# A hybrid streaming encoder step on one core: other assumed times in the scheduler that orders its instructions

## The chip, the core and the metric

The kernel runs on one core of a Trainium2 chip. The metric is the device time of one execution in microseconds (us), the median of several runs. A core has five engines that run beside each other, each through its own instructions in a fixed order: PE (TensorE, the matmuls; PEld is its loading of weights), DVE (VectorE), ACT (ScalarE), POOL (GpSimd) and SP (SyncE, which here issues nearly all DMAs). An instruction that needs another engine's result waits on a semaphore, and what stands behind it on its own engine waits with it.

## The reference, cut to what matters

One layer (DEPTH is 1) over 64 new frames of a running stream and over 16 meta tokens and 2048 prompt frames of a new one, 1024 features wide:

```python
hn = rms_norm(x, prm['norm_mix_g'][l])
proj = hn @ prm['w_in'][l]
aq, ak, av, lx, lg, gq, gk, gv, glr, gog = jnp.split(proj, split_points, axis=-1)
...
o_att = diff_attention_prompt(q, k.reshape(b, L, ATT_HEADS, 2, ATT_DH), v, lam)
...
hseq, lru_h1 = rg_lru(xc, lru_h0, ...)
o_lru = hseq * jax.nn.gelu(lg)
...
o_gla, S1 = gla_blocked(...)
o_gla = rms_norm(o_gla.astype(dt), prm['gla_norm_g'][l]).reshape(b, L, GLA_VW) * jax.nn.silu(gog)
x = x + jnp.concatenate([o_att, o_lru, o_gla], axis=-1) @ prm['w_out'][l]
hn = rms_norm(x, prm['norm_ffn_g'][l])
u = hn @ prm['ffn_w_up'][l]
uc, ffn_c1 = causal_dwconv(u, ffn_c0, prm['ffn_conv_w'][l], prm['ffn_conv_b'][l])
x = x + (jax.nn.gelu(uc) * (hn @ prm['ffn_w_gate'][l])) @ prm['ffn_w_down'][l]
```

A final norm follows. Differential attention has 4 heads with two score maps each (exponentials, normalised, one subtracted from the other), and its keys reach back over all chunks. The LRU and the gated linear attention (GLA) are recurrences along the frames. The feed-forward part (FFN) is 2816 wide.

## The kernel before

**Layout.** Features lie on the partitions and the 2128 frames in the columns. Each large matmul is done as three products in a rounded 32-bit type: high part by high part, high by low, low by high (names end in h and l, or hi and lo). So each weight tile `raw` must first be split: ACT rounds it to `whi` (L154), and POOL (L261) or DVE (L160) takes the difference `wlo`. That happens on first use; both parts are then stored in DRAM (`WS`) and read back for later groups of columns.

**Three streams** are written by generators that take turns in `Flow.run` in fixed shares (1680, 564 and 640), which makes the order of the program's text:

- dense: the input projection in six blocks of columns (`ps_w`, L645 and L647), each with a norm ahead of it; then the FFN in four groups of columns, 512, 512, 512 and 336+256. A group is the output projection (`pd`, L1435), the residual add with a sum of squares, a norm, then per FFN tile the products up and gate (`pu`, `pg`, L1302), the convolution and GELU on DVE, ACT and POOL (L1314 to L1339), the rounding to `gh` (L157), and the product down (`pd`, L1369) with the add to x on DVE (L1375).
- attention: the scores of a unit (`ps_sc`, L1056 to L1063), their minimum on DVE (L1065) and the exponential on ACT (L1066), in two PSUM buffers; a mixing of the two maps (`pc`: a multiply on POOL, L157, then one on DVE, L1104, that also adds); and PV: transposes (`ps_pt`, L1155), a split into `ph` (ACT, L154) and `pl` (DVE, L160), the products with V (`ps_o`, L1170), and a norm over each head (`osq`, `ps_on`, `dgt`, L1185 to L1196). Its instructions have a priority 500 ahead of dense.
- recurrent: LRU (L712 to L767) and GLA (L789 to L960), also 500 ahead.

A group of the FFN may begin only when the attention and recurrent chunks that it needs are done. Between the last product down of one group and the output projection of the next, TensorE also runs the final norm of the first of them. The last group (336+256) runs when both mixers are through.

**A norm** is the same chain everywhere: squares summed by a matmul (`ps_sq`, L397), a multiply-add on DVE (L420), a power on POOL (L421), a diagonal matrix `dg` on DVE (L426), and a matmul that spreads it over the partitions (`ps_nb`, L432). Then come y (DVE, L439), its rounding to `h2h` (ACT, L154) and the difference `h2l` (DVE L160 or POOL L444), on which the next matmuls of dense wait. What keeps TensorE busy meanwhile is work of the two mixers that stands between L397 and the next dense matmul:

```python
for w, a, b in runs(cuts):
    nc.vector.tensor_scalar(r[:w, a:b], ps[:w, a:b], 1.0 / D, EPS, ALU.mult, ALU.add)
nc.gpsimd.tensor_tensor(out=r[:, :len(cuts)], in0=r[:, :len(cuts)], in1=mhalf[:, :len(cuts)], op=ALU.pow)
```

**What sets the order on the engines** is not the text alone. The program is built under `tile.TileContext(nc, schedule_with_timeline_sim=True)`. That scheduler runs through the program on assumed times: on each engine, of the instructions whose inputs are there by its assumed clock, it places the one with the best priority (the place in the text, less 500 for the mixers, 50000 for a norm of the FFN, 100000 for the setup). The result is one fixed list of instructions for each engine with its waits. At run time nothing is reordered. The assumed times come from a table of constants, `TRN2Spec`: `CYCLE_T` holds the nanoseconds of one cycle of DVE, ACT and POOL, and `PE_FULL_CLOCK_PASS_GAP_NS` (2.5 before) is what a matmul takes beyond one column for each cycle at the full clock.

## Time and profile before

| | |
|---|---|
| median of 3 runs | 2969.09 us (2964.97 to 2972.47) |
| profiled execution, its own time | 2967.71 us |
| its span in the trace | 2965.9 us |
| mean granted TensorE clock | 0.98 |
| busy: PE, DVE, ACT, POOL | 2840.8, 1892.6, 1097.0, 759.3 us |
| DMA | 669.92 MB, mean 226 GB/s |

The span runs from the first to the last instruction on the slowest core (here the only one); the time of the execution holds 1.8 us more. Busy time of PE counts its pipelined matmuls with modelled ends, so that it also holds time in which TensorE ran at half clock or drained between dependent steps.

### The profile page before, as it was taken

To read this page: it belongs to the slowest core of one execution; us is meant where nothing else is said; L and a number is where in the kernel's file an instruction comes from. 1 tells how busy PE (TensorE), PEld (TensorE's weight loads), DVE (VectorE), ACT (ScalarE), POOL (GpSimd) and SP (SyncE) were. 2 spreads that over 40 slices of the span, in tenths; PEclk is the share of its full clock that TensorE was granted. 3 is DMA by queue.
4 is the path that set the end of the run, shared out by engine and by line. 5 is a ranking of instruction groups with operands and counts; after the bars stand their busy time and mean duration, and the time that the engine had idled before them with its cause. 6 is when DMAs were issued, how large, how long until landed. Compare 5 with 4: busy or idle time off the path is not lost.

```text
span 2965.9 us, 44899 instructions
## 1 busy us (share of the span) xinstructions
PE 2840.8 (96%) x16031; PEld 2501.3 (84%) x16031; DVE 1892.6 (64%) x3798; ACT 1097.0 (37%) x2525; POOL 759.3 (26%) x1162
## 2 busy tenths in 40 slices
PE   6998999999899999998999999999999999999998
PEld 6988999999777877877787888877888889999998
DVE  6467656564578898899687687766565445433334
ACT  5344443442444454554343343334332112211112
POOL 4224312221245445444222212223021101100001
PEclk9998999999899999999999999999999999999999
DMA  9997677787967787887575665685555764434443
GB/s 327 324 272 215 228 259 218 234 272 229 337 234 252 262 277 255 263 263 246 196 236 187 202 210 194 217 288 192 195 193 191 259 219 156 171 142 171 146 167 134
DMA packets 314942, 669.92 MB, mean 226 GB/s; under 512 B 35127, under 2 KB 174143, under 8 KB 314719
## 3 DMA queue, kind: packets, MB, share of 16 engines
q1 hardware_dynamic: 314574, 667.05, 67.1%
q8 instruction: 127, 2.08, 0.3%
q14 instruction: 97, 0.79, 0.1%
q10 hardware_dynamic: 144, 0.01, 0.0%
HBM read 491.99 MB, written 174.96 MB: 225 GB/s over the span
## 4 chain that ended last, share of the span: by engine, by line
PE 48%; DVE 5%; DMA 2%; POOL 1%; issue 1%; ACT 1%; SPq 0%; POOLq 0%; ACTq 0%; DVEq 0%
PE pd L1369 13%; PE pg L1302 12%; PE pu L1302 12%; PE pd L1435 4%; PE ps_o L1170 2%; DMA whi<-WS 2%; PE ps_pt L1155 1%; PE ps_sc L1063 1%; PE ps_sc L1056 1%; DVE pc L1104 1%; POOL pc L157 1%; DVE y L439 0%; PE ps_r L895 0%; DVE cc L1326 0%; DVE x L1375 0%
## 5 line engine op out<-in xcount | busy, mean ns | idle before, releaser
L1066 ACT ACTIVATE pc<-ps_sc,NB 128x512 f32<-128x512 f32 (+6 forms) x400 | 224.1, 562 | 298.2 <-DVE NB L1065 284.4
L1369 PE MATMUL pd<-gh,whi 128*128 128x512 f32 (+2 forms) x880 | 319.0, 366 | 11.0 <-DVE x L1375 5.0
L1302 PE MATMUL pu<-h2h,whi 128*128 128x512 f32 (+2 forms) x880 | 318.9, 362 | 6.9 <-DVE cc L1337 4.5
L1302 PE MATMUL pg<-h2h,whi 128*128 128x512 f32 (+2 forms) x880 | 317.3, 361 | 4.7 <-DMA whi<-WS 3.6
L1302 PE MATMUL pu<-h2l,whi 128*128 128x512 f32 (+2 forms) x880 | 317.0, 360 | 0.5 <-DVE h2l L160 0.4
L1302 PE MATMUL pg<-h2l,whi 128*128 128x512 f32 (+2 forms) x880 | 316.3, 359 | 0.0
L1302 PE MATMUL pu<-h2h,wlo 128*128 128x512 f32 (+2 forms) x880 | 316.2, 359 | 0.0
L1302 PE MATMUL pg<-h2h,wlo 128*128 128x512 f32 (+2 forms) x880 | 315.2, 358 | 0.0
L1369 PE MATMUL pd<-gh,wlo 128*128 128x512 f32 (+2 forms) x880 | 313.0, 357 | 0.0
L1369 PE MATMUL pd<-gl,whi 128*128 128x512 f32 (+2 forms) x880 | 312.9, 358 | 0.0
L1375 DVE TENSOR_TENSOR x<-x,pd 128x512 f32<-128x512 f32 (+2 forms) x360 | 222.4, 623 | 139.1 <-PE pd L1369 136.6
L1326 DVE SCALAR_TENSOR_TENSOR cc<-uh,prm,cc 128x512 f32<-128x512 f32 (+4 forms) x264 | 174.7, 667 | 180.2 <-ACT cc L1324 176.8
L1065 DVE TENSOR_REDUCE NB<-ps_sc 128x1 f32<-128x512 f32 (+6 forms) x400 | 208.2, 530 | 102.3 <-PE ps_sc L1063 101.0
L645 PE MATMUL ps_w<-hh,whi 128*128 128x384 f32 (+2 forms) x768 | 260.7, 341 | 12.6 <-ACT whi L154 9.7
L645 PE MATMUL ps_w<-hh,wlo 128*128 128x384 f32 (+2 forms) x768 | 261.2, 341 | 8.7 <-DVE wlo L160 5.3
L645 PE MATMUL ps_w<-hl,whi 128*128 128x384 f32 (+2 forms) x768 | 258.0, 337 | 0.0
L1319 ACT ACTIVATE uh<-pu 128x512 f32<-128x512 f32 (+4 forms) x132 | 59.2, 463 | 382.5 <-PE pu L1302 381.0
L261 POOL TENSOR_TENSOR wlo<-raw,whi 128x1024 fp32r<-128x1024 f32 (+2 forms) x63 | 151.6, 2407 | 169.8 <-ACT whi L154 152.0
L1369 PEld LDWEIGHTS pd<-gh,whi 128*128 128x128 f32 x880 | 165.5, 189 | 34.8 <-DVE x L1375 7.5
L1302 PEld LDWEIGHTS pu<-h2h,whi 128*128 128x128 f32 x880 | 167.7, 191 | 29.5 <-DVE cc L1337 5.3
L157 POOL TENSOR_SCALAR gh<-cc 128x512 fp32r<-128x512 f32 (+4 forms) x132 | 68.7, 523 | 483.5 <-DVE cc L1339 299.5
L157 POOL TENSOR_SCALAR pc<-pc,fr 128x512 f32<-128x512 f32 (+4 forms) x200 | 159.1, 813 | 123.7 <-DVE fr L1086 106.2
(330 smaller groups left out, 6975.6 us busy)
## 6 DMA issues: line engine op xcount, KB each, us to landing
whi<-WS SPq DMA_DIRECT2D x276, 512.0 KB
wlo<-WS SPq DMA_DIRECT2D x276, 512.0 KB
WS<-whi SPq DMA_DIRECT2D x94, 512.0 KB
WS<-wlo SPq DMA_DIRECT2D x94, 512.0 KB
Kc<-KHL SPq DMA_DIRECT2D x48, 512.0 KB
V<-VHL SPq DMA_DIRECT2D x48, 512.0 KB
Q<-QHL SPq DMA_DIRECT2D x64, 256.0 KB
raw<-in_wu SPq DMA_DIRECT2D x22, 512.0 KB
```

The costliest lines, as they stand in the source:

```text
L157: nc.gpsimd.tensor_scalar(out, in_, s, 1.0, ALU.mult, ALU.mult)
L261: nc.gpsimd.tensor_tensor(out=lo[:, :n], in0=t[:, :n], in1=f(hi[:, :n]), op=ALU.subtract)
L645: nc.tensor.matmul(ps[:, :n], lhsT=wx, rhs=hx, start=st_, stop=sp_)
L1065: nc.vector.tensor_reduce(NB[:qw, ti, m, ci:ci + 1], ps[:qw, :kt_], AX.X, ALU.min)
L1066: nc.scalar.activation(out=pv_[m][:qw, :kt_], in_=ps[:qw, :kt_], func=AF.Exp, scale=-1.0, bias=NB[:qw, ti, m, ci:ci + 1], accum_out=SS[:qw ...
L1170: nc.tensor.matmul(oT, lhsT=V[:kw, b0 // P, a, :], rhs=r[:kw, i, :], start=(first and i3 == 0), stop=(fin and i3 == 2))
L1302: nc.tensor.matmul(ps[:, :n], lhsT=w_[wi_][:, k * P:(k + 1) * P], rhs=hx, start=(k == 0 and i3 == 0), stop=(k == KT - 1 and i3 == 2))
L1319: nc.scalar.activation(out=uh[:, 2:2 + m], in_=pu[:, a:b], func=AF.Copy)
L1326: nc.vector.scalar_tensor_tensor(out=cc[:, :m], in0=uh[:, w:w + m], scalar=cw[w], in1=cc[:, :m], op0=ALU.mult, op1=ALU.add)
L1369: nc.tensor.matmul(ps[:, :n], lhsT=w_, rhs=g_[:, o:o + n], start=(j == 0 and i3 == 0), stop=(j == len(gts) - 1 and i3 == 2))
L1375: nc.vector.tensor_tensor(x2[b, ct], x2[b, ct], ps[:, :n], ALU.add)
L1435: nc.tensor.matmul(ps[:, :n], lhsT=w_, rhs=g_, start=(k == 0 and i3 == 0), stop=(k == KT - 1 and i3 == 2))
```

## The change

Ahead of everything else, the module now writes four numbers of the scheduler's table: the cycle of DVE 1.4 times as long as it was, that of ACT 1.15 times, that of POOL 1.2 times, and 13 ns in place of 2.5 beyond the columns of a matmul. Nothing else differs, and every later line has a number 9 higher.

```diff
+from concourse.hw_specs import TRN2Spec
 from concourse.masks import make_identity
+
+
+TRN2Spec.CYCLE_T = {
+    mybir.EngineType.DVE: 1.4 * TRN2Spec.CYCLE_T[mybir.EngineType.DVE],
+    mybir.EngineType.Activation: 1.15 * TRN2Spec.CYCLE_T[mybir.EngineType.Activation],
+    mybir.EngineType.Pool: 1.2 * TRN2Spec.CYCLE_T[mybir.EngineType.Pool],
+}
+TRN2Spec.PE_FULL_CLOCK_PASS_GAP_NS = 13.0
```

Both programs hold the same instructions (15731 rows of PE in either). What differs is the order on each engine. Written as a difference of the two lists, 4787 rows of PE, 2957 of DVE, 1638 of ACT, 560 of POOL and 779 of SP stand elsewhere, most of them by a few places. Three places follow, of the kernel before and then of the changed one.

**ScalarE at the start.** The input projection's first column blocks run here: `whi` is the rounding of a weight tile that TensorE waits for, `sp_b` and `l1p` belong to the setup of the LRU, `sq` to the squares of the next block's norm, `acc` (L407, L416) to its end, `ckr` to the cached keys. Before:

```order
L349 ACTIVATE l1p<-sp_b 128x2
L154 ACTIVATE whi<-raw 128x1024
L154 ACTIVATE ckr<-ck 128x512
L154 ACTIVATE whi<-raw 128x1024
L407 ACTIVATE acc<-ps_nb 128x384
L712 ACTIVATE xc<-lx,prm 128x83
L154 ACTIVATE hh_0_346<-y 128x384 x3
L154 ACTIVATE whi<-raw 128x1024
```

And changed:

```order
L347 ACTIVATE sp_b<-sp_b 128x2
L391 ACTIVATE sq<-xt 128x384
L163 ACTIVATE whi<-raw 128x1024
L358 ACTIVATE l1p<-sp_b 128x2
L163 ACTIVATE ckr<-ck 128x512
L163 ACTIVATE whi<-raw 128x1024
L721 ACTIVATE xc<-lx,prm 128x83
L163 ACTIVATE whi<-raw 128x1024
L736 ACTIVATE tt<-ps_r,hb 128x83
L743 ACTIVATE tt<-tt,nsp_192 128x83
L416 ACTIVATE acc<-ps_nb 128x384
```

The last `whi` shown stands ahead of `acc` and of four steps on `hh` where it stood behind them, and the first one stands ahead of `l1p`.

**GpSimd at the final norm of the second FFN group,** ahead of the output projection of the third (about 1955 us in the trace before). `r_20961` and `dgt` belong to the norm of an attention head, `r` with L421 (L430) is the dense stream's norm, `pc` the mixing of the attention's two maps. Before:

```order
L214 TENSOR_SCALAR r_20961<-r_20961 128x2
L215 TENSOR_TENSOR r_20961<-r_20961,mhalf 128x2
L157 TENSOR_SCALAR dgt<-ident,r_20961 128x128 x2
L421 TENSOR_TENSOR r<-r,mhalf 128x4
L157 TENSOR_SCALAR pc<-pc,fr 128x512 x6
L157 TENSOR_SCALAR pc<-pc,fr 128x384 x2
L157 TENSOR_SCALAR pc<-pc,fr 128x16
L157 TENSOR_SCALAR pc<-pc,fr 128x144
```

And changed:

```order
L223 TENSOR_SCALAR r_20961<-r_20961 128x2
L224 TENSOR_TENSOR r_20961<-r_20961,mhalf 128x2
L166 TENSOR_SCALAR dgt<-ident,r_20961 128x128 x2
L166 TENSOR_SCALAR pc<-pc,fr 128x512 x6
L166 TENSOR_SCALAR pc<-pc,fr 128x384 x2
L166 TENSOR_SCALAR pc<-pc,fr 128x16
L166 TENSOR_SCALAR pc<-pc,fr 128x144
L430 TENSOR_TENSOR r<-r,mhalf 128x4
```

Ten mixings that stood behind the dense norm's power now stand ahead of it.

**TensorE at the same norm.** `ps_sq` (L397, L406) sums the squares, `ps_nb` (L432, L441) spreads the result, `pd` (L1435, L1444) is the next dense step; the rest is attention and GLA. Before:

```order
L1063 MATMUL ps_sc<-Kc,Q 128x144
L1056 MATMUL ps_sc<-Kc,Q 128x144
L1061 LDWEIGHTS mq
L1061 MATMUL ps_sc<-mk,mq 128x64
L1063 MATMUL ps_sc<-Kc,Q 128x144
L1185 MATMUL ps_on<-ones,osq 128x1 x2
L397 MATMUL ps_sq<-ones,acc 128x1 x4
L1194 MATMUL ps_on<-dgt,ones 128x256
L432 MATMUL ps_nb<-dg,ones 128x512
L1435 MATMUL pd<-h2h_20338,whi 128x512
```

And changed (`ps_sq` stands eleven rows above the first row shown):

```order
L923 MATMUL ps_r<-S_p,qkd 128x256
L925 MATMUL ps_r<-gvr,att 128x64 x4
L1179 MATMUL ps_o<-pl,V 128x256
L1179 MATMUL ps_o<-ph,V 128x256 x2
L1179 MATMUL ps_o<-pl,V 128x256
L1164 MATMUL ps_pt<-ident,pc 128x128 x4
L1065 MATMUL ps_sc<-Kc,Q 128x512
L1072 MATMUL ps_sc<-Kc,Q 128x512
L930 MATMUL ps_r<-gvr,qkd 128x256
L441 MATMUL ps_nb<-dg,ones 128x512
L1444 MATMUL pd<-h2h_20338,whi 128x512
```

Nineteen rows of attention and GLA stand between `ps_sq` and `ps_nb`, where before one stood there.

**TensorE at the second norm of the last group** (about 2507 us), where no mixer is left. `pu` and `pg` are the group's first up and gate products over its block of 336 columns; the norm is that of its block of 256. Before:

```order
L432 MATMUL ps_nb<-dg,ones 128x256
L432 MATMUL ps_nb<-dg,ones 128x80
L397 MATMUL ps_sq<-ones,acc 128x1 x2
L1302 MATMUL pu<-h2h_24682,whi 128x336
L1302 MATMUL pg<-h2h_24682,whi 128x336
L1302 MATMUL pu<-h2l_24683,whi 128x336
L1302 MATMUL pu<-h2h_24682,wlo 128x336
L1302 MATMUL pu<-h2h_24682,whi 128x336
```

And changed:

```order
L441 MATMUL ps_nb<-dg,ones 128x256
L441 MATMUL ps_nb<-dg,ones 128x80
L406 MATMUL ps_sq<-ones,acc 128x1 x2
L1311 MATMUL pu<-h2h_24682,whi 128x336
L1311 MATMUL pg<-h2h_24682,whi 128x336
L441 MATMUL ps_nb<-dg,ones 128x256
L1311 MATMUL pu<-h2l_24683,whi 128x336
L1311 MATMUL pu<-h2h_24682,wlo 128x336
```

The `ps_nb` of the block of 256 columns stands two matmuls behind its `ps_sq`; before, 26 matmuls stand between them.

## Rows read from the trace of the kernel before

**Rows 1.** The page: busy time of each engine, two of its lines of 40 slices (tenths; 9 is 90% or more), and the shares of the chain of waits by engine.

```profile
PE 2840.8 (96%) x16031; PEld 2501.3 (84%) x16031; DVE 1892.6 (64%) x3798; ACT 1097.0 (37%) x2525; POOL 759.3 (26%) x1162
...
PEclk9998999999899999999999999999999999999999
DMA  9997677787967787887575665685555764434443
...
PE 48%; DVE 5%; DMA 2%; POOL 1%; issue 1%; ACT 1%; SPq 0%; POOLq 0%; ACTq 0%; DVEq 0%
```

**Rows 2.** The chain of waits in order of time, in the last quarter: start, duration, work: 24 matmuls of 512 columns.

```profile
2338.63 5.44 PE pu L1302 x24
```

**Rows 3.** Windows of the core: stretch in us, its length, then busy us and instructions of PE, PEld, DVE, ACT and POOL, the granted clock, the DMA share, GB/s. The first goes from the end of the input projection to the first output projection; the others hold the norm ahead of the FFN in group 0, the final norm of group 0, the norm ahead of the FFN in group 1, the final norm of group 1, and the norm ahead of the FFN in group 2.

```profile
768.00:804.00 36.00, 27.76 (x121) 21.10 (x121) 23.34 (x48) 16.24 (x41) 8.95 (x14) 0.72 1.01 365
846.00:864.00 18.00, 12.51 (x48) 8.26 (x47) 16.19 (x41) 8.06 (x20) 9.95 (x13) 0.77 0.86 277
1381.00:1395.00 14.00, 12.07 (x81) 10.34 (x79) 13.86 (x42) 7.29 (x22) 2.58 (x3) 1.00 0.63 200
1448.00:1462.00 14.00, 13.74 (x88) 11.79 (x87) 12.05 (x26) 10.39 (x25) 5.42 (x8) 1.00 0.56 179
1951.00:1963.00 12.00, 7.43 (x32) 5.11 (x30) 9.83 (x24) 3.38 (x12) 7.81 (x12) 0.67 0.76 221
2018.00:2029.00 11.00, 10.12 (x66) 7.96 (x65) 7.71 (x18) 6.38 (x18) 1.22 (x2) 1.00 0.51 157
```

**Rows 4.** The same view of the start, and of the rest of the input projection.

```profile
27.00:75.00 48.00, 33.38 (x166) 30.58 (x167) 38.07 (x76) 22.98 (x44) 28.71 (x29) 0.85 0.92 311
75.00:110.00 35.00, 31.97 (x180) 31.01 (x179) 10.73 (x23) 11.36 (x20) 8.49 (x4) 0.86 0.99 342
110.00:760.00 650.00, 630.34 (x4201) 599.28 (x4200) 391.14 (x933) 273.45 (x746) 169.96 (x264) 0.99 0.78 249
```

**Rows 5.** The timeline of PE: the last matmul of the projection and the first of the output projection of group 0.

```profile
768.65 0.28 PE L645 MATMUL ps_w<-hh,wlo 128*128 128x256 f32 x1
...
797.77 0.63 PE L1435 MATMUL pd<-h2h,whi 128*128 128x512 f32 x1
```

**Rows 6.** What scores (L1056) and PV (L1170) waited for on TensorE over the whole span: us in total, times, the longest.

```profile
PE ps_o L1170 <- DVE pl L160: 8.1, 8, 2.9
PE ps_sc L1056 <- ACT pc L1066: 7.9, 11, 2.7
PE ps_o L1170 <- ACT ph L154: 6.6, 6, 2.5
```

**Rows 7.** The timeline of ACT at the start (start, duration, line, work, and in brackets the idle time ahead of it and what ended it), then a row of PE there.

```profile
32.21 0.20 ACT L349 ACTIVATE l1p<-sp_b 128x2 f32<-128x2 f32 x1 [4.20 <-DVE sp_b L346]
...
73.17 0.34 ACT L753 ACTIVATE lgt<-lgt 128x160 f32<-128x160 f32 x1 [1.58 <-DVE lgt L752]
73.42 0.87 ACT L154 ACTIVATE whi<-raw 128x816 fp32r<-128x816 f32 x1
...
74.34 0.51 PE L647 MATMUL ps_w<-whi,hh 128*80 128x272 f32 x1 [5.16 <-ACT whi L154]
```

**Rows 8.** The timeline at the final norm of the second group: POOL, then PE.

```profile
1955.01 0.19 POOL L214 TENSOR_SCALAR r<-r 128x2 f32<-128x2 f32 x1 [7.03 <-DVE fr L1080]
...
1956.79 1.02 POOL L421 TENSOR_TENSOR r<-r,mhalf 128x4 f32<-128x4 f32 x1
1957.80 7.73 POOL L157 TENSOR_SCALAR pc<-pc,fr 128x512 f32<-128x512 f32 x10
...
1952.04 0.23 PE L1056 MATMUL ps_sc<-Kc,Q 128*128 128x144 f32 x1
...
1954.62 1.58 PE L397 MATMUL ps_sq<-ones,acc 128*128 128x1 f32 x8
...
1961.29 2.07 PE L432 MATMUL ps_nb<-dg,ones 128*128 128x512 f32 x2 [3.19 <-DVE dg L426]
1962.37 1.41 PE L1435 MATMUL pd<-h2h,whi 128*128 128x512 f32 x1
```

**Rows 9.** The timeline at the second norm of the last group: PE, DVE, POOL.

```profile
2506.65 0.61 PE L397 MATMUL ps_sq<-ones,acc 128*128 128x1 f32 x4 [0.58 <-DVE acc L384]
...
2513.65 0.59 PE L432 MATMUL ps_nb<-dg,ones 128*128 128x256 f32 x2
...
2511.69 0.47 DVE L426 TENSOR_SCALAR dg<-ident,r 128x128 f32<-128x128 f32 x2
...
2509.32 0.98 POOL L421 TENSOR_TENSOR r<-r,mhalf 128x2 f32<-128x2 f32 x1
```

**Rows 10.** Groups by line and shape: names, shapes, count, busy us, mean ns of one, idle us before them. First DVE: the minimum of a score step, the mixing, and a step of the FFN's convolution that multiplies and adds on the same shape. Then ACT: the exponential of a score step.

```profile
L1065 DVE TENSOR_REDUCE NB<-ps_sc 128x1 f32<-128x512 f32 x192 | 129.5, 683 | 45.2 <-PE ps_sc L1063 44.8
...
L1104 DVE SCALAR_TENSOR_TENSOR pc<-pc,fr 128x512 f32<-128x512 f32 x96 | 95.2, 1022 | 8.4 <-POOL pc L157 8.2
...
L1339 DVE SCALAR_TENSOR_TENSOR cc<-uh,cc 128x512 f32<-128x512 f32 x44 | 30.2, 687 | 2.2
...
L1066 ACT ACTIVATE pc<-ps_sc,NB 128x512 f32<-128x512 f32 x192 | 131.3, 685 | 160.3 <-DVE NB L1065 157.0 <-DVE dg L862 2.8
```

## The prediction

> **What bounds the kernel now.** I read the page first. [rows 1] PE is busy 96% of the span and leads the chain of waits; no other engine passes 64%, and DMA is full only in the first quarter. So the time is TensorE's: its streaming, plus what it loses in waits and at half clock. The chain in order of time shows the streaming undisturbed [rows 2]: 24 matmuls of 512 columns in 5.44 us, 226.7 ns each. At the upper clock of 2.4 GHz 512 columns are 213.3 ns, so 13.3 ns stand beyond the columns. Priced so, all matmuls of the program come to about 2765 us (an estimate of mine over the list of TensorE). The span is 2965.9, so about 200 us are lost; no edit of an order can give back anything else.
>
> Where they are lost I read from the windows. [rows 4] From 27 to 75 us PE is busy 33.4 of 48 at clock 0.85, from 75 to 110 the clock is 0.86, and then 650 us run at 0.99 and 97% busy: the start loses, the long projection hardly does. [rows 3] After it come stretches in which dense waits for a chain through POOL, DVE and ACT: clock 0.72 in 768 to 804, 0.77 in 846 to 864, 0.67 in 1951 to 1963; three others keep clock 1.00 since enough mixer work stands in them. [rows 6] The rest are waits of about a microsecond between TensorE and the attention's other engines.
>
> **What the change removes and adds: nothing.** No instruction, byte or buffer differs; each term below is work that stands elsewhere. Does the plan become truer? For matmuls yes: 13 ns assumed against 13.3 seen [rows 2], where 2.5 made TensorE 11 ns too fast, 2 to 5% of a matmul. The Trainium skill ("TensorE: Matmul & The Clock Gate", section "Wait — 56ns, not 53.3ns?") gives 2.5 ns as the fixed cost of one matmul at the upper clock, 215.7 ns at 512 columns. By it the streaming would be at most 170 us less than my 2765 (15731 rows by 11 ns), the loss that much greater, and the new plan would assume too slow a TensorE; this trace disagrees with its 226.7 ns, and the measurement decides.
>
> For DVE one factor fits no single row: the same shape takes 687 ns at L1339 and 1022 at L1104, 1.49 times as long, where POOL multiplies the next `pc` beside it [rows 10]. So the plan comes nearer in one place and goes further off in another; and a truer plan is not by itself a faster list. I go place by place.
>
> *Start.* On ACT, `whi` roundings move ahead of other work. Two delays of before show what this is worth. L349 sat 4.20 us on a DVE result with a `whi` right behind it in ACT's list; and the 816-wide `whi` at 73.42 stood behind L753, which had waited 1.58 for DVE, while TensorE sat 5.16 us on that `whi` [rows 7]. In the changed list both stand ahead of these steps. The gain reaches from 0 to 9 us (5.16, plus most of the 4.20). But in 27 to 75 us the DMA share is 0.92 and in 75 to 110 it is 0.99 [rows 4]: an earlier rounding frees its buffer earlier, yet the next load can use only the idle 8% of 48 us, 3.8 us. I take **−4**.
>
> *End of the projection, 768 to 804.* Dense waits until attention and recurrence have finished their early chunks. From 768.8 to 797.8 [rows 5] TensorE has 14.7 us of mixer work by columns, so about 14 us are lost, 0.97 for each of work. In the changed list 11.1 us are left there, 3.6 having gone ahead into the projection, where they fill a busy TensorE at no loss: **−4**, between 0 (DMA share is 1.01 there, so a load could set the end [rows 3]) and −6.
>
> *Norm gaps.* For each I count the TensorE work that stands between the dense step ahead and the one behind. In 846 to 864 it is 7.0 before and 7.3 now: 0. In 1381 to 1395 it falls from 10.9 to 7.3, and a gap that the chain sets loses what it lacks in filling: **+4**, at least 0. In 1448 to 1462, 12.5 and 12.2: 0. In 2018 to 2029, 7.8 and 7.8: 0. In 1951 to 1963 it rises from 3.0 to 11.1. Before, the gap lasts from 1952.0 to 1962.4, 7.4 us of it lost. [rows 8] But POOL now places ten `pc` mixings, 7.73 us in the trace, ahead of the norm's L421, so the chain grows: from `ps_sq` at 1954.62 to `ps_nb` at 1961.29 were 6.7 us; now 7.7 + 1.0 for L421 + 3.5 from its end to `ps_nb`, about 12, with some 3 us of work in the gap ahead of `ps_sq`. So 15 long with 11.1 of work, 3.9 lost: **−4**, from −7 (mixings done in POOL's 7.03 us of idleness) to +3 (the mixings wait for DVE as long as L214 did).
>
> *Second norm of the last group.* Its `ps_nb` now stands two matmuls behind `ps_sq`. L421 ended at 2510.30 and `dg` could follow at once instead of at 2511.69, so TensorE would stand from about 2508.5 to 2510.8; nothing of the mixers is left to fill it. [rows 9] **+2**, from 0 to +3.
>
> *Tight places.* For each wait of TensorE on another engine I take the TensorE work between it and the TensorE step whose result that engine needed. Over both lists, those with less than 2 us are 119 before and 179 now; outside the stretches above 4 and 15. Their price: of scores (L1056) and PV (L1170) 39 have under 1.5 us before, and these lines waited 8.1 + 7.9 + 6.6 = 22.6 us in 25 waits [rows 6], 0.58 for each tight place. Eleven more outside the stretches: **+6**, from 0 to +7. Those inside (66 before, 110 now) I leave at nothing, because the chain of the stretch runs at the same time; if that cover is gone, 44 × 0.45 would be 20.
>
> The sum: −4 − 4 + 4 − 4 + 2 + 6 = 0. The profiled execution took 2967.7 and lies 1.4 below the median, so I expect **2969 us**, no change. The ends of the known terms add to −26 and +17; not all come together.
>
> **The rivals.** *Faster, about 2946.* The stretches are filled and the clock follows: at clocks 0.72, 0.77 and 0.67 PE was busy 27.8, 12.5 and 7.4 us [rows 3], of which 0.28, 0.23 and 0.33 would go at full clock, 7.8 + 2.9 + 2.5 = 13. With the start at −9, that is −22, other terms cancelling. For it: the low clock stands exactly where TensorE sat idle, and the matmul gap is right now. Against: 768 to 804 is not filled but shorter, and in 846 to 864 nothing changes.
>
> *Slower, about 2994.* The place is the attention's ring of scores and PV inside the stretches of 768 to 900 and 1376 to 1470. There are two score buffers; a score step of 512 columns is two matmuls, 0.45 us of TensorE by [rows 2], but 0.68 on DVE and about as long on ACT [rows 10]. Where the changed list puts scores one after the other (as in its rows at the final norm of the second group), TensorE runs at their pace, and dense behind it too, since nothing is reordered at run time. 44 tight places by 0.45 and the 11 outside by 0.45 are +25. It decides as soon as the other engines' chain is longer than the norm's, so that tight places add to a stretch instead of filling it. For it: tight places grow by half, and 22.6 us were lost so before. Against: mixer work that fills a stretch costs nothing until the norm is done.
>
> *The change does nothing to the order:* excluded, since the difference of TensorE's two lists has 4787 rows.
>
> **How the numbers follow.** Chances: no change 0.36 (about 2961 to 2978), faster 0.33, slower 0.31. Measurement of this kernel can tell about 0.3%, 9 us, from no change; the three chances are the same cases by that bound. As both signs hold more together than the likeliest, the range must reach both rivals: 2944 to 2996. The forecast's own would be 2960 to 2979.
>
> **What would show it.** In the changed profile: start right, if TensorE's wait for an 816-wide `whi` is gone and the projection's end comes some 8 us earlier; wrong, if TensorE waits there on DMA instead. The gap near 1951 should show clock near 1.00 and POOL's `pc` ahead of L430; the one near 1381 a clock below 1.00. The waits for `pc`, `pl` and `ph` on L1065 and L1179 should add to about 29 us; if they come to 45 or more, the slower rival holds. If these stay near 23 and the stretch at 768 to 900 is some 10 us shorter, the faster one does. My count of work per gap says nothing of when the other engines arrive; that is where the forecast can fail in either direction.

## The result: 1.04% slower

| | before | changed |
|---|---|---|
| median of 4 runs | 2967.93 us | 3000.82 us (2992.64 to 3003.09) |
| ratio to before, 95% interval | | 1.0104 (1.0081 to 1.0128) |
| span of the profiled execution | 2965.9 us | 2997.3 us |
| mean granted TensorE clock | 0.980 | 0.973 |

The forecast was 2969 us, no change; the time lies above the range of 2944 to 2996 and near the slower rival's 2994. This is the busy line of the page of the changed kernel, which answers to the first of [rows 1]:

```profile
PE 2858.0 (95%) x16031; PEld 2514.3 (84%) x16031; DVE 1893.6 (63%) x3798; ACT 1089.6 (36%) x2525; POOL 757.7 (25%) x1162
```

The span is 31.4 us longer. TensorE's busy time grew by 17.2 us with the same matmuls, while its granted clock fell from 0.980 to 0.973, and its idle time (span less busy) grew by 14.2 (139.3 against 125.1). DVE, ACT and POOL are as busy as before to within 8 us.

What TensorE waited for in the changed kernel, over the whole span (us in total, times, the longest), the answer to [rows 6]:

```profile
PE ps_sc L1065 <- DMA Q<-QHL: 26.8, 12, 4.6
PE ps_w L654 <- ACT whi L163: 19.9, 6, 6.9
PE ps_sc L1065 <- ACT pc L1075: 15.5, 19, 2.0
PE ps_o L1179 <- ACT ph L163: 8.0, 16, 1.8
...
PE ps_o L1179 <- DVE pl L169: 4.9, 4, 2.9
```

The first row is new at the top. In the kernel before, the same view has it so:

```profile
PE ps_sc L1056 <- DMA Q<-QHL: 5.4, 5, 1.6
```

TensorE's waits for a load of Q grew by 21.4 us, which is more than its idle time as a whole did. The row below it lies at the start, in the first 110 us, which are faster all the same (below). Scores waiting for ScalarE grew by 7.6 (15.5 against 7.9); all other idle time together fell by about 15.

**What Q is.** A unit of attention is one head of one chunk of queries. Its queries lie in one buffer (`Q = mp.tile(..., bufs=1)`), filled by two DMAs from DRAM. So the load of the next unit's Q can be issued only when the last score matmul of the unit ahead has run, and the next unit's first score must wait for it to land. What hides the load is other TensorE work that the list puts in between. Here is one such place in the changed kernel, TensorE's timeline and then SyncE's, which issues the loads:

```profile
1399.37 0.31 PE L1072 MATMUL ps_sc<-Kc,Q 128*128 128x144 f32 x1
...
1401.25 0.38 PE L1164 MATMUL ps_pt<-ident,pc 128*16 128x128 f32 x2
1406.27 0.79 PE L1065 MATMUL ps_sc<-Kc,Q 128*128 128x512 f32 x1 [4.64 <-DMA Q<-QHL]
```

```profile
1398.95 0.37 SPq L157 DMA_DIRECT2D V<-VHL  x1
1399.71 1.24 SPq L157 DMA_DIRECT2D Q<-QHL  x2
1401.00 0.60 SPq L157 DMA_DIRECT2D Kc<-KHL  x1
```

At 1399.37 the last score on the old Q starts; at 1399.71 the two loads are issued, at once, behind a load of V; at 1406.27 the first score on the new Q starts, after 4.64 us in which TensorE did nothing. From the last use to the first use are 6.9 us, and the list had 0.9 us of work there. The windows of the changed kernel around this place (stretch, length, then busy us of PE, PEld, DVE, ACT, POOL, clock, DMA share, GB/s):

```profile
1399.00:1402.00 3.00, 1.78 (x10) 0.99 (x8) 3.00 (x9) 2.00 (x9) 0.00 (x0) 1.00 1.03 391
1402.00:1406.30 4.30, 0.03 (x1) 0.03 (x1) 1.67 (x5) 0.32 (x2) 0.00 (x0) 0.65 1.05 242
1406.30:1412.00 5.70, 5.70 (x17) 4.18 (x17) 2.46 (x8) 1.38 (x4) 0.85 (x1) 0.50 0.03 13
1412.00:1420.00 8.00, 8.00 (x26) 5.52 (x25) 7.45 (x19) 4.51 (x12) 4.48 (x7) 0.69 0.44 146
```

The DMA share is 1.03 and 1.05 while Q is on its way: Q shares the DMA engines with V and Kc, issued beside it. And the wait is paid twice. After it TensorE is busy all the time, for 5.7 us at a clock of 0.50 (its lower level, 1.2 GHz) and for 8 us at 0.69, where it had 1.00 ahead of the wait: 5.7 × 0.50 + 8 × 0.31 = 5.3 us more, by estimate, behind a wait of 4.64.

Over both lists I took, for the 35 reloads, the TensorE work between the last use and the next first use (columns ÷ 2.4 GHz + 13 ns, an f32 matmul counted as four: the two 128-column transposes at 1398.76 in the changed kernel take 0.39 us up to the next matmul). In the changed kernel, 14 of these places show TensorE idle by over 0.5 us just ahead of the first score, and from last use to first use are 5.4 to 9.8 us there; the profile puts 11 of these waits down to Q, one to a load of K, and of two it shows no releaser. Where there is less work than some 5.5 us, TensorE mostly stands. Before, 4 of 35 places have less than 5 us, now 13; the shortfall below 5.5 us, summed, is 11.9 us before and 32.2 now. This sum is called the shortfall below; it is an estimate, and counting the work a little otherwise moves it by some 2 us.

Three stretches of the changed kernel that answer to [rows 3], in the columns of the windows above, and ahead of them the one in which the first small units follow each other:

```profile
225.00:262.00 37.00, 27.13 (x117) 22.93 (x117) 22.93 (x65) 13.34 (x49) 7.33 (x13) 0.63 0.54 146
775.00:800.70 25.70, 18.37 (x73) 13.27 (x71) 18.36 (x38) 12.26 (x32) 7.26 (x10) 0.70 1.04 347
1396.20:1416.20 20.00, 14.30 (x55) 10.07 (x53) 13.13 (x41) 7.48 (x25) 1.71 (x2) 0.68 0.60 176
1976.00:1998.10 22.10, 16.35 (x72) 12.25 (x71) 19.95 (x41) 9.26 (x23) 12.99 (x17) 0.85 0.50 158
```

That first stretch in the kernel before:

```profile
225.00:262.00 37.00, 31.51 (x164) 28.25 (x162) 32.17 (x87) 14.26 (x51) 15.86 (x29) 0.78 0.60 181
```

From 225 to 262 us the clock is 0.63 where it was 0.78, and PE is busy 27.1 of 37 us where it was 31.5: three reloads of Q stand there with 4.5, 0.7 and 1.2 us of work.

### The profile page after: what moved, and what is told of

It reads as the page before. It is cut to its first block, busy times and chain, and to the rows that moved or that the text cites. A ratio compares the mean times of both kernels' runs of the same rounds, so it can differ in the third digit from the quotient of the medians.

```text
span 2997.3 us, 44933 instructions
## 1 busy us (share of the span) xinstructions
PE 2858.0 (95%) x16031; PEld 2514.3 (84%) x16031; DVE 1893.6 (63%) x3798; ACT 1089.6 (36%) x2525; POOL 757.7 (25%) x1162
## 2 busy tenths in 40 slices
DMA packets 314942, 669.92 MB, mean 224 GB/s; under 512 B 35127, under 2 KB 174143, under 8 KB 314719
## 4 chain that ended last, share of the span: by engine, by line
PE 77%; DMA 10%; DVE 8%; ACT 2%; issue 2%; POOL 1%; SPq 1%; POOLq 0%; ACTq 0%; DVEq 0%
PE pu L1311 15%; PE pg L1311 15%; PE pd L1378 15%; PE ps_w L654 8%; PE pd L1444 6%; PE ps_o L1179 4%; PE ps_w L656 3%; PE ps_sc L1065 2%; PE ps_sc L1072 2%; DMA Q<-QHL 2%; PE ps_pt L1164 2%; PE ps_r L904 1%; DVE pc L1113 1%; DMA raw<-in_wi 1%; DMA wlo<-WS 1%
## 5 line engine op out<-in xcount | busy, mean ns | idle before, releaser
L654 PE MATMUL ps_w<-hh,whi 128*128 128x384 f32 (+2 forms) x768 | 260.5, 341 | 20.1 <-ACT whi L163 19.9
L163 ACT ACTIVATE ph<-ps_pt 128x512 fp32r<-128x512 f32 (+1 forms) x192 | 100.3, 522 | 287.8 <-PE ps_pt L1164 274.4
L1065 PE MATMUL ps_sc<-Kc,Q 128*128 128x512 f32 (+6 forms) x400 | 155.4, 388 | 50.0 <-DMA Q<-QHL 26.8
```

Of the source, the lines that this page charges most:

```text
L163: nc.scalar.activation(out=out, in_=in_, func=AF.Copy, scale=scale)
L654: nc.tensor.matmul(ps[:, :n], lhsT=wx, rhs=hx, start=st_, stop=sp_)
L1065: nc.tensor.matmul(ps[:qw, :kt_], lhsT=Q[:, 0, m, qo:qo + qw], rhs=Kc[:, m, :kt_], start=True, stop=False)
```

## The experiments

Two theories on the extra time. **Q**: it comes from reloads of the one Q buffer that the list no longer hides, and follows the shortfall. **T**: it comes from the tight places of the prediction (waits of TensorE with less than 2 us of its own work since the step that feeds them), 119 before, 180 now (179 by the prediction's count). All lists hold the same instructions unless the text says otherwise; tight places and shortfall are counts over the lists. "Before" is the old kernel timed on the same chip, 2967.9 to 2970.5 us in all comparisons.

| run | median us | ratio to before (95%) | shortfall | tight | wait for Q, us |
|---|---|---|---|---|---|
| kernel before | 2968 | 1 | 11.9 | 119 | 5.4 |
| changed kernel | 3000.82 | 1.0104 (1.0081 to 1.0128) | 32.2 | 180 | 26.8 |
| e1: 13 ns alone | 2987.20 | 1.0052 (1.0037 to 1.0067) | 11.4 | 103 | 6.9 |
| e2: DVE and 13 ns | 2965.45 | 0.9980 (0.9970 to 0.9989) | 13.5 | 197 | 14.4 |
| e3: ACT, Pool and 13 ns | 2979.85 | 1.0035 (1.0022 to 1.0048) | 21.1 | 116 | 15.5 |
| e4: all four, DMA 2.5 us later in the plan | 2945.86 | 0.9918 (0.9902 to 0.9934) | 11.7 | 192 | 2.7 |
| e5: old numbers, Q loaded once | 2947.09 | 0.9927 (0.9900 to 0.9954) | none | 133 | 0 |
| e6: all four, Q loaded once | 2941.75 | 0.9910 (0.9887 to 0.9932) | none | 174 | 0.2 |
| e7: old numbers, DMA 2.5 us later | 2937.06 | 0.9892 (0.9871 to 0.9914) | 3.2 | 144 | 0 |
| e8: all four, DMA 3.5 us later | 2960.75 | 0.9977 (0.9961 to 0.9993) | 6.7 | 192 | 3.3 |
| e9: 13 ns, DMA 2.5 us later | 2950.48 | 0.9938 (0.9922 to 0.9954) | 6.7 | 117 | 3.5 |
| e10: three cycles, DMA 2.5 us later | 2944.92 | 0.9923 (0.9904 to 0.9942) | 6.9 | 199 | 0.2 |
| e11: old numbers, DMA 1.5 us later | 2954.68 | 0.9953 (0.9938 to 0.9968) | 2.9 | 119 | 0.9 |
| e12: 13 ns, Q loaded once | 2960.57 | 0.9968 (0.9956 to 0.9980) | none | 117 | 0 |

e1 to e8 were timed on one chip and e9 to e12 on another, each beside the kernel before; across the two, compare the ratios.

### Parts of the change, e1 to e3

The numbers that a run doesn't name keep their old value:

```diff
# e1
+TRN2Spec.PE_FULL_CLOCK_PASS_GAP_NS = 13.0
# e2
+    mybir.EngineType.DVE: 1.4 * TRN2Spec.CYCLE_T[mybir.EngineType.DVE],
+TRN2Spec.PE_FULL_CLOCK_PASS_GAP_NS = 13.0
# e3
+    mybir.EngineType.Activation: 1.15 * TRN2Spec.CYCLE_T[mybir.EngineType.Activation],
+    mybir.EngineType.Pool: 1.2 * TRN2Spec.CYCLE_T[mybir.EngineType.Pool],
+TRN2Spec.PE_FULL_CLOCK_PASS_GAP_NS = 13.0
```

Expected of e1: 

> Only the 13 ns of a matmul are assumed, the cycles of the other engines are as before. Theory Q: the loss comes from the one buffer of Q. Between the last score matmul on a unit's Q and the first on the next unit's, the reload takes about 5.5 us, and what TensorE work the list puts there falls short of it by 11.9 us in sum over 35 reloads before, by 32.2 in the changed kernel. Here it is 11.4, so 2968, within 6 us of before, and TensorE's wait for Q at 5 to 9 us. Theory T (tight places): the loss follows the number of waits of TensorE with less than 2 us of its own work since the step that feeds them, 119 before, 180 in the changed kernel, 33 us for 61. Here they are 103, so 2968 - 9 = 2959.

Expected of e2: 

> DVE 1.4 and 13 ns, ScalarE and Pool as before. Theory Q: the shortfall is 13.5 us against 11.9 before, so 2970, within 8 us, and the wait for Q below 10 us. Theory T: 197 tight places against 119, 78 x 0.54 = +42, so 3010.

Expected of e3: 

> ScalarE 1.15, Pool 1.2 and 13 ns, DVE as before. Theory Q: the shortfall is 21.1 us against 11.9, about 1.3 us lost for each (27 us of wait for 20.3), +12, so 2980, and the wait for Q near 18 us. Theory T: 116 tight places, no more than before, so 2966.

e2 and e3 tell the theories apart, and both go against T. e2 has the most tight places and is no slower than before (2965, where T said 3010 and Q 2970). e3 has fewer tight places than before and is 10 us slower (T 2966, Q 2980). Q's wait in e2 and then in e3, from the same view as above:

```profile
PE ps_sc L1064 <- DMA Q<-QHL: 14.4, 9, 4.4
```

```profile
PE ps_sc L1064 <- DMA Q<-QHL: 15.5, 8, 5.2
```

Both times lie where Q put them, but e2's wait is 14.4 us where Q said below 10. (That profile is of the slowest of e2's ten executions, 2974.6 us.) Some other gain must cover it in e2; no run shows which. e1 is a miss of both: 2987 where they said 2968 and 2959, and its wait for Q is small. What grew most in e1 is a wait in the GLA, 2.6 us in five times before (L895):

```profile
PE ps_r L898 <- DVE att L902: 10.7, 4, 5.3
...
PE ps_sc L1059 <- DMA Q<-QHL: 6.9, 5, 4.0
```

### The plan told that DMAs come later, e4

```diff
+TRN2Spec.DGE_DMA_DELAY = {k: v + 2500 for k, v in TRN2Spec.DGE_DMA_DELAY.items()}
```

This constant is what the scheduler assumes between the issue of a DMA and the start of its copy; nothing on the chip changes. The four numbers of the change stay.

Expected of e4: 

> All four numbers of the change, and in the plan alone a DMA starts 2.5 us later. Theory Q: the plan now knows that Q comes late; the shortfall is 11.7 us as before, with tight places as many as in the changed kernel (192 of 180), so the wait for Q falls from 27 to below 10 us and the time to about 2975. Theory T: 192 tight places, so 3000 or more.

```profile
PE ps_sc L1065 <- DMA Q<-QHL: 2.7, 3, 1.4
```

The wait for Q went from 26.8 to 2.7 us, with as many tight places as in the changed kernel, and the time fell by 55 us to 2946. T is refuted: it said 3000 or more. Q's direction is confirmed and its size isn't, since it forecast 2975; the DMA constant gives more than what the changed kernel had lost. So e4 alone doesn't show how much of its 55 us is Q's.

### Q loaded once, e5 and e6

```diff
-        Q = mp.tile([P, 2, 2, 256], F32R, tag="Q", name="Q", bufs=1)
-        for half in range(2):
-            ld(out=Q[64 * half:64 * half + 64, :, :, :nq],
-               in_=QHL[h, :, :, :, u.tok0:u.tok0 + nq].rearrange("l m d c -> d l m c"))
+        if not Q_once:
+            Q_once.append(mp.tile([P, 2, 2, 256], F32R, tag="Q", name="Q", bufs=1))
+            for half in range(2):
+                ld(out=Q_once[0][64 * half:64 * half + 64],
+                   in_=QHL[0, :, :, :, 0:256].rearrange("l m d c -> d l m c"))
+        Q = Q_once[0]
```

Expected of e5: 

> Leaves out: Q is loaded once, for the first unit, and every later unit's scores use that Q, so no score waits for a reload (71 of 72 loads of Q are gone). Old assumed times. Theory Q: the kernel before waited 5.4 us for Q, so 2970 - 5 to - 9 = 2961 to 2965. Rival R (what the new numbers cost lies elsewhere, in the ring of scores and PV or in the order of the other engines): the same here.

Expected of e6: 

> The same with the four new numbers. Theory Q: the changed kernel loses its 27 us of wait, 3001 - 27 to - 35 = 2966 to 2974, within 10 us of the run before with Q loaded once, or below it, since the order of the other engines gains about 24 us over the kernel before when Q's delay is in the plan. Rival R: it stays 25 us or more above that run, 2987 or more.

These kernels leave out the reloads: every unit's scores use the first unit's queries. (One load is two DMAs, so 70 of the 72 are gone, not 71; the core moves 653.00 MB where it moved 669.92.) The busy lines of the pages of e5, then of e6, whose spans are 2944.3 and 2942.5 us:

```profile
PE 2834.0 (96%) x16031; PEld 2495.7 (85%) x16031; DVE 1895.6 (64%) x3798; ACT 1095.7 (37%) x2525; POOL 755.4 (26%) x1162
```

```profile
PE 2841.8 (97%) x16031; PEld 2501.1 (85%) x16031; DVE 1888.7 (64%) x3798; ACT 1089.3 (37%) x2525; POOL 763.3 (26%) x1162
```

With no reload to wait for, the four numbers together cost nothing: 2941.75 against 2947.09 without them, and the two intervals overlap. In the changed kernel the reloads were worth 59 us (3000.8 − 2941.8), in the one before 21 (2968 to 2947), so the difference, 38, covers the whole loss of 33. Rival R, which wanted 2987 for e6, is refuted. Q's own forecasts were missed in size, by 14 us in e5 and by 24 in e6: both runs gain more than the waits for Q. The profiled executions of the changed kernel and e6 are 54.8 us apart, 38.6 of it idle time (139.3 to 100.7) and 16.2 busy time with the same matmuls (2858.0 to 2841.8). The wait itself is 26.8; how the rest divides between what follows from it and what other lists and less DMA traffic give, these runs don't show. A second buffer for Q, which would keep all work, doesn't fit beside the kernel's pools, so no run has it.

### Where the gain of the late DMA comes from, e7 to e11

e7 is e4 without the change's four numbers, e8 is e4 with 3500 in place of 2500, e9 has the 13 ns alone of the four, e10 the three cycles alone, and e11 is e7 with 1500.

Expected of e7: 

> Old assumed times and only the start of a DMA 2.5 us later in the plan. Theory Q alone: the shortfall is 3.2 us against 11.9, so about 11 us below before, 2959. Rival D (the gain of the run with all four numbers and the late DMA comes from the DMA number alone): 2946. If the four numbers carry part of that gain, this stays at 2955 to 2962, and the run with both is faster by 10 us or more.

Expected of e8: 

> All four new numbers and a DMA start 3.5 us later in the plan. Theory Q: the shortfall is 6.7 us against 11.7 with 2.5 us, so 2946 - 6 = 2940. Theory T: tight places 192 as with 2.5, so 2946; if the wait for Q was already nothing with 2.5 us (2.7 us measured), nothing more is to be had and other orders decide within 10 us.

Expected of e9: 

> 13 ns for a matmul and a DMA start 2.5 us later in the plan, cycles as before. The 13 ns alone cost 17 us with a wait for Q of only 6.9 us, which theory Q did not foresee. If that loss too hangs on DMAs that come later than planned, this run is near the one with old numbers and the late DMA, 2937 + 1.3 x (6.7 - 3.2) = 2941. If it is a loss of another kind (rival O: TensorE behind VectorE in the GLA and the scores), it stays, 2954.

Expected of e10: 

> The three longer cycles without the 13 ns, and a DMA start 2.5 us later in the plan. Theory Q: shortfall 6.9 us, so about 2942, between the old numbers (2937, 3.2) and all four (2946, 11.7). If the longer cycles cost something of their own, 2950 or more; if they gain, below 2937.

Expected of e11: 

> Old numbers, a DMA start 1.5 us later in the plan in place of 2.5. Shortfall 2.9 us against 3.2, tight places 119 against 144. Theory Q: the same as with 2.5 us, 2937. If the size of the delay itself matters, half of the gain is left, 2950.

e7 is the fastest of all, 1.08% below the kernel before, and its gain needs none of the four numbers: rival D holds (it said 2946, for 2937 measured), and with the late DMA all four cost some 9 us (e4 against e7). Its page's busy line, and its stretch of the small units, which stood at a clock of 0.78 before and 0.63 in the changed kernel:

```profile
PE 2828.5 (96%) x16031; PEld 2495.2 (85%) x16031; DVE 1895.9 (65%) x3798; ACT 1091.9 (37%) x2525; POOL 767.4 (26%) x1162
```

```profile
225.00:262.00 37.00, 34.39 (x198) 31.46 (x196) 27.40 (x70) 19.00 (x54) 24.25 (x37) 0.91 0.80 256
```

The clock there is 0.91 now and PE is busy 34.4 of 37 us. But the shortfall doesn't order these runs: e11 has 2.9 and takes 2955, e4 has 11.7 and takes 2946, e8 has 6.7 and takes 2961, where 2940 was expected. So below a shortfall of some 12 us other things in the lists decide, by 12 us either way among the runs with a late DMA (2937 to 2961), and e1, with 11.4, took 2987. Of Q's forecasts of a time for e1 to e8, e10 and e11, three come within 8 us (e2, e3, e10): its sign holds, a fixed price for each us of shortfall doesn't. That the delay works through more loads than Q's would fit: TensorE's waits for all other loads are 8.0 us in e7, 15.1 in e11 and 13.5 before. It isn't shown apart.

### The 13 ns alone, with no reload, e12

The edit of e5 with that of e1.

Expected of e12: 

> Leaves out the same as the two runs with Q loaded once; 13 ns assumed for a matmul, cycles as before. If the 17 us of the 13 ns hang on Q, it falls to the others, 2942 to 2948. If they are a loss of another kind, 2955 to 2965.

Against the list with the old numbers, the 13 ns cost 17 us in e1, 13 in e9 (against e7) and 13 in e12 (against e5). (The last two pairs are of two chips; by their ratios to before it is 14 and 12.) In these two TensorE waits for Q 3.5 us at most, so this loss is of another kind, as rival O said. Where O puts it, behind VectorE, the waits do grow, from 46.6 us in e7 to 53.2 in e9 and from 44.9 in e5 to 50.9 in e12, but hardly in the GLA (2.9 to 3.3 and 5.2 to 6.3); the rest is open. Beside longer cycles it is gone: e4 with the 13 ns and e10 without are 2946 and 2945. That TensorE, assumed slower, makes the other engines look relatively quick in the plan, and longer cycles undo that, would fit; it is argued and not shown.

## Why the prediction was wrong

**The failed step is one that isn't in the sum: the loads that a moved instruction waits for.** The prediction counted a wait as tight when less than 2 us of TensorE work stood behind the step that feeds it. It counted waits on other engines; waits of scores for loads stand at nothing in the sum, with no reason given. For Q the feeder is a DMA that can start only when TensorE itself has let the buffer go, and where TensorE stood, 5.4 to 9.8 us passed from the last use to the first. Of the 35 places 13 have under 5 us of work now, and 8 of these have over 2 us, so the bound of 2 us wouldn't have caught them either. What the runs showed in its place: 26.8 us of waits for Q against 5.4, with half clock behind them. Those 5.4 us, in the same view as [rows 6], were the row to ask "what if this is longer".

The terms of the sum, by TensorE's time up to the same matmul of the dense stream, in both traces:

- *Start, −4*: the size is right, the mechanism in part. Dense stands 5.1 us earlier at 93 us. The steps moved as read: `l1p` no longer holds a `whi` (the next one, at 37.82, waits for its load, as the prediction said it might), and the 816-wide `whi` that stood behind L753 no longer does; it is the second of that width, now at 65.36, and TensorE's wait for it fell from 5.16 to 1.98 us. But up to 110 us TensorE's waits for any `whi` grew, from 14.9 to 21.9, so the gain came from elsewhere too: waits for `wlo` fell from 8.6 to 3.8, those of the LRU's products from 3.6 to nothing. And the prediction's sign, the projection's end some 8 us earlier, failed: its last matmul starts at 775.01 for 768.65, 6.4 us later. ACT's timeline in the changed kernel, then TensorE's row:

```profile
34.85 0.20 ACT L358 ACTIVATE l1p<-sp_b 128x2 f32<-128x2 f32 x1 [3.44 <-DVE sp_b L355]
...
37.82 1.06 ACT L163 ACTIVATE whi<-raw 128x1024 fp32r<-128x1024 f32 x1 [1.91 <-DMA raw<-in_wi]
...
65.36 0.87 ACT L163 ACTIVATE whi<-raw 128x816 fp32r<-128x816 f32 x1
...
66.28 0.35 PE L656 MATMUL ps_w<-whi,hh 128*80 128x272 f32 x1 [1.98 <-ACT whi L163]
```

- *End of the projection, −4*: the shortening was right (25.7 us against 29.1, for 3.6 us less work), the term wrong. The gap shrank by as much as the work that left it, so the loss stayed at 14.5 us: 0. The price of 0.97 for each us of work was the mistake; that work had cost nothing in it.
- *Final norm of group 0, +4*: gap 19.9 us against 13.9, loss 12.6 against 3.0: +9.6. The sign and the lacking work are right, and the clock is below 1.00 as forecast (0.68), but the wait of 4.64 us for Q stands in this gap, with the half clock behind it.
- *Final norm of group 1, −4*: the work in it is 11.0 us as counted, but the gap is 22.1 where 15 were expected: +3.4, beyond the worse end of the term. The clock there is 0.85 where near 1.00 was forecast. A wait of 1.5 us for Q stands in it; how much the ten `pc` steps ahead of the norm and the scores in it add wasn't tried apart.
- *Other norms, 0*: within 1.3 us. *Last group, +2*: +0.9.
- *Tight places, +6*: right in sum, by luck in place. Scores and PV waited 15.5 + 8.0 + 4.9 = 28.4 us on ACT and DVE where 29 were forecast. The term was for places outside the stretches, and those inside stood at nothing. But from 768 to 940 us these waits grew from 9.8 to 15.9 us, and everywhere else they went from 12.8 to 12.5.

The terms for the start, the end of the projection and the norms, as measured, come to about +9 of the 31 us; the rest lies where the sum had tight places alone. Take as loss the time between two dense matmuls less the TensorE work that the list puts there (priced as for the shortfall; an estimate). From 110 to 262 us of the trace before it went from 28 to 34, from 864 to 960 from 14 to 25, and from 1462 to 1952 from 4 to 13. In the first and the last stand waits for Q of 11.7 and 4.1 us. In the middle one stands none; there scores waited 5.5 us for ScalarE where they had waited 0.2, so at this place the slower rival's mechanism does show, first in the changed kernel and then before:

```profile
PE ps_sc L1065 <- ACT pc L1075: 5.5, 4, 1.9
```

```profile
PE ps_sc L1056 <- ACT pc L1066: 0.2, 1, 0.2
```

From 960 to 1372 the changed kernel gained 5. In e6 the three are 17, 17 and 3. (The lower ends of the prediction's terms, as listed, add to −22, not −26.)

The time came near the slower rival's 2994 mostly by another way than its mechanism: its mark was 45 us or more of such waits, and they are 28.4. The experiments refute it as the cause of the whole: e2, with 197 tight places, is no slower than before, and e4, with 192, is faster. What it had right is that a list can make TensorE wait with dense behind it. The clock was in the prediction only as a gain of the faster rival; here it doubled the price of a wait.

The four numbers also took something off: apart from the waits of scores for ScalarE and for Q, TensorE's idle time fell by about 15 us, and with Q's reloads taken out the changed kernel is no slower.

## What to carry to other kernels

When a scheduler's order changes, look at each buffer that has only one copy and is filled by a DMA: take the work that the engine has between the last use of the old content and the first of the new, and set it against the time from last use to first use that the trace shows where the engine waited. A table of assumed times should be mended where the program's waits hang on it; here the engines' cycles and the matmul gap moved the time by −5 to +33 us, and the assumed start of a DMA, 2.5 us later, took 1.08% off with the old numbers. More faithful numbers for some engines may lose: here they lost 33 us as long as the plan had the loads start as early as it did, and the 13 ns alone lost 13 even with late loads or with no reload.

## What the runs showed that was not expected

- A wait of 4.64 us of TensorE was followed by 5.7 us at a granted clock of 0.50 and 8 us at 0.69, by estimate 5.3 us lost on top of it.
- A load of 0.5 MB in two DMAs, issued at once beside 0.5 MB loads of V and Kc, took 6.9 us from last use to first use at a DMA share of 1.03 to 1.05; the 14 places in which TensorE stood ahead of the first score took 5.4 to 9.8 us.
- 13 ns beyond a matmul's columns agree with the trace's 13.3, and yet a plan with 13 is 13 to 17 us slower than one with 2.5 in three pairs of runs, and as fast beside longer cycles (e4, e10). Why is open.
